# Seven products per pair of weight slabs: a new order of the products, their sums handed out one per step, and the last product in a bank of its own

## The chip, the cores and the metric

The kernel runs on one core of a Trainium2 chip. The metric is device time of one launch in microseconds (us). TensorE (PE) does the matrix products, VectorE (DVE) and ScalarE (ACT) the elementwise work, GpSimd (POOL) and SyncE (SP) issue transfers; each engine works through its own list of instructions in order.

## The reference

It is one inference step of a two-layer decoder trunk, for a prompt of 512 tokens and 8 x 8 sample tokens that share all weights (576 columns in all). Layer A is a convolution module, layer B a dilated attention. The part that matters here is the projection that feeds layer B's queries and the shared keys:

```python
h = jnp.einsum('btd,de->bte', x, w_in)        # B layer: queries, gate, memory queries, ...
q, gate, qm, gm = jnp.split(h, [MIX_WIDTH, MIX_WIDTH + B_OUT, MIX_WIDTH + B_OUT + MEM_WIDTH], axis=-1)
kv = jnp.einsum('btd,de->bte', x, w_kv_shared).reshape(b, t, 2, N_GROUPS, B_HEADS_PER_GROUP, HEAD_DIM)
```

with x of 576 x 2048 and each head a block of 128 output rows. All is float32.

## The kernel before

A product of weights by activations is done a slab at a time: 128 output rows by 2048 inputs. A slab is loaded, cast on ACT into a rounded high part `wh` (L349), and DVE takes the remainder as the low part `wl` (L360); the product is hi·hi + hi·lo + lo·hi.

Of the 24 query and key slabs of layer B, the first four are done plainly (steps `n_fill` to `n_pairs`, 16 steps of 24 matmuls), and the other 20 in ten pairs (steps `n_pairs` to `n_rest`). A pair is a 2 x 2 block product (two slabs, two halves of the 2048 inputs, two halves of 288 columns) done by Strassen's scheme in Winograd's form: seven products in place of eight, at the price of sums. The sums of the activations (tiles `comb`, made on DVE in L1173 and L1180 and on ACT in L1179) are made once, in `combine`. The sums of the weights are made for each pair: s3 = a − c (L187), s2 = d − s3 (L189), s4 = b − s2 (L193) and s1 = c + d (L197), where a and b are the two halves of the first slab and c and d those of the second; each comes in two quarters, 0 and 1, of 128 x 512.

A pair has 14 steps: 7 products, two quarters each. A step is 12 matmuls of 288 columns (L224 the eight on `wh`, L227 the four on `wl`). The results go to two PSUM tiles of two banks each: `self.x` holds the banks A and Dd, `self.y` the banks B and E. Products whose results are added stand in one bank, and what is needed before the bank goes on is copied out by `after` into the three parts s0, s1 and s2 of the tile `snap`, or is evacuated with one of them added (`ev_qk`, L1280 to L1292). `after` of a step is called at the end of the step behind it, that is behind that step's matmuls in the program.

`manual_schedule` means that each engine's instructions stand in the order in which this Python code calls them. At the end of step i, `run_steps` casts weights for the steps up to i + 3 (`issue_hi`), makes low parts up to i + 2 (`issue_split`), loads what has room (`issue_pairs`), calls `after`, and does background work from `bg` as far as the budget `state["avail"]` goes. The budget grows with the matmuls of a step and by `extra`, and is limited to `cap`. Before the pairs start, what is left of `bg` is done in one go (`while bg: one_bg()`).

The raw quarters `rawq` of a pair lie in twelve slots (eight in `qpool`, four others), loaded on SP's queue in the order of `LOADS`. Copies of caches from memory to memory (`copy_some`, L502) are also issued on SP's queue, by hooks at given steps. Behind the pairs come the value, memory and gate slabs of layer B (steps `n_rest` to `n_b`, 24 matmuls each), with sample attention beside them in a lane (`samples`), which reads cache chunks `kv` that POOL loads (L480) and whose first matmuls are in L1421.

Of the kernel before, what the change touches and what calls it, by code (L numbers as in the profile page):

```python
# [14 lines left out]
OP = mybir.AluOpType  # L15
# [66 lines left out]
def trunk(ctx, tc, xt, memt, wm, wa, wao, wb, wbo, cst, scv, kc, rest, mc, relb, oneh,  # L82
          o_y, o_yf, o_cp, o_cs, o_kv, o_kvn, o_kc, o_rest, o_mem):
    nc = tc.nc
# [56 lines left out]
    class Pair:  # L141
# [2 lines left out]


        spare = None
        LOADS = ("a0", "a1", "b0", "b1", "c0", "d0", "c1", "d1")
        PRODUCTS = (("a", "b11"), ("b", "b21"), ("s2", "t2"), ("s3", "t3"), ("s1", "t1"), ("d", "t4"), ("s4", "b22"))

        def __init__(self, slabs, move, evs, scale):  # L150
            self.slabs, self.move, self.evs, self.scale = slabs, move, evs, scale
# [22 lines left out]
        def free(self, name):  # L174
            slots[self.slot.pop(name)] += 1

        def operand(self, i):

            w, g, _ = self.sets[i]
            g = str(g)  # L180
            r = self.raw
            first = self.qi[0]
            if w == "s2" and "s3" + g not in r:
                issue_split(first + int(g) + 1)
                slots["due"] -= 1
                r["s3" + g] = n = self.take("n" + g)
                nc.vector.tensor_tensor(n, r["a" + g], r["c" + g], op=OP.subtract)  # L187
                r["s2" + g] = r.pop("a" + g)
                nc.vector.tensor_tensor(r["s2" + g], r["d" + g], n, op=OP.subtract)  # L189
            if w == "s3" and "s4" + g not in r:  # L190
                issue_split(first + 4 + int(g) + 1)
                r["s4" + g] = r.pop("b" + g)
                nc.vector.tensor_tensor(r["s4" + g], r["s4" + g], r["s2" + g], op=OP.subtract)  # L193
                self.free("a" + g)
            if w == "s1" and "s1" + g not in r:
                r["s1" + g] = r.pop("c" + g)
                nc.vector.tensor_tensor(r["s1" + g], r["s1" + g], r["d" + g], op=OP.add)  # L197
            return r[w + g]

        def done(self, i):  # L200

            w, g, _ = self.sets[i]
            slot = {"s3": "n", "s1": "c", "d": "d", "s4": "b"}.get(w)
            if slot:
                self.free(slot + str(g))

        def emit(self, i):
            if i == 0:
                self.x = new_pp()
                self.st = wpool.tile([128, 1024], F32, tag="raw", bufs=2, name=f"snap{names[0]}")  # L210
                slots["raw"] += 1
            if i == 6:
                self.y = new_pp()
            A, Dd, B, E = ((t_, c) for t_ in (self.x, getattr(self, "y", None)) for c in range(2))
            w, g, x = self.sets[i]
            t_, c = {"a": A, "b": Dd, "s2": A, "s3": B, "s1": A, "d": E, "s4": A}[w]
            hi, lo = splits[self.qi[i]]
            o = t_[:, c, 0:288]
            fresh = w in ("a", "b", "s3", "d") and g == 0
            for kk in range(4):  # L220
                if w in ("a", "b"):
                    y_ready(g * 4 + kk + (8 if w == "b" else 0), None)
                for part in range(2):
                    nc.tensor.matmul(o, hi[:, kk * 128:(kk + 1) * 128], self.move(x, g * 4 + kk, part),  # L224
                                     start=(fresh and kk == 0 and part == 0), stop=False, skip_group_check=True)
            for kk in range(4):
                nc.tensor.matmul(o, lo[:, kk * 128:(kk + 1) * 128], self.move(x, g * 4 + kk, 0), start=False,  # L227
                                 stop=(g == 1 and kk == 3), skip_group_check=True)

        def after(self, i):  # L230

            w, g, _ = self.sets[i]
            if g == 0:
                return
            sc = self.scale
            s0, s1, s2 = (self.st[:, j * 288:(j + 1) * 288] for j in range(3))
            A, Dd = (self.x[:, c, 0:288] for c in range(2))
            if w == "a":
                nc.scalar.activation(s0, A, AF.Copy, scale=sc)
            elif w == "b":  # L240
                self.evs[0](0, Dd, s0)
            elif w == "s2":
                nc.scalar.activation(s1, A, AF.Copy, scale=sc)
            elif w == "s3":
                nc.vector.scalar_tensor_tensor(s0, self.y[:, 0, 0:288], sc, s1, op0=OP.mult, op1=OP.add)
            elif w == "s1":
                nc.scalar.activation(s2, A, AF.Copy, scale=sc)
                self.evs[1](1, self.y[:, 0, 0:288], s2)
            elif w == "d":
                self.evs[1](0, self.y[:, 1, 0:288], s0)  # L250
                slots["raw"] -= 1
            else:
                self.evs[0](1, A, None)

    slots = dict(q=0, u=0, due=0, raw=0)
    steps, quarters, halves = [], [], []
# [38 lines left out]
    def issue_pairs():  # L295

        while state["dma"] < len(halves) and isinstance(halves[state["dma"]][0], Pair):
            un, name = halves[state["dma"]]
            if "q" not in scopes or slots["q"] + slots["u"] <= slots["due"] + (0 if un.raw else 2):
                return  # L300
            un.load(name)
            state["dma"] += 1
# [89 lines left out]
    def run_steps(upto=None):  # L392
        upto = len(steps) if upto is None else upto
        while state["pos"] < upto:
            i = state["pos"]
            un, q, cs, last = steps[i]
            pair = isinstance(un, Pair)
            if not pair and not hasattr(un, "ps"):
                un.ps = new_pp()
            qi = un.qi[q]  # L400
            issue_split(qi + 1)
            issue_dma(quarters[qi][2] + (6 if "s" in scopes else 4 if un.spare else 2))
            hi, lo = splits[qi]
            if pair:
                un.emit(q)
            for kk in range(0 if pair else 4):
                k = (q * 4 + kk + un.flip) % un.nk
                if un.ready:
                    for c in cs:
                        un.ready(k, c)  # L410
                w = (hi[:, kk * 128:(kk + 1) * 128], lo[:, kk * 128:(kk + 1) * 128])
                for a, (wi, xs) in enumerate(((0, un.hi), (0, un.lo), (1, un.hi))):
                    for c in cs:
                        c0, n = un.chunks[c]
                        nc.tensor.matmul(un.ps[:, c, :n], w[wi], xs[k][:, c0:c0 + n],  # L415
                                         start=(q == kk == a == 0),
                                         stop=(last and kk == 3 and a == 2 and not un.tail))
            if last and un.tail:
                un.tail(un.ps)
            state["avail"] += (288 if pair else sum(un.chunks[c][1] for c in cs)) * 12 / 2400 + state["extra"]  # L420
            for f in hooks.pop(i, []):
                f()
            top = max(v.qi[w_] for v, w_, _, _ in steps[i:i + 4]) + 1
            issue_hi(top)
            issue_split(max(v.qi[w_] for v, w_, _, _ in steps[i:i + 3]) + 1)
            if cstate["use"]:
                chunk_load()
            issue_pairs()
            if i and isinstance(steps[i - 1][0], Pair):
                steps[i - 1][0].after(steps[i - 1][1])  # L430
            elif i and steps[i - 1][3]:
                finish_evac()
            stage_lanes()
            state["avail"] = min(state["avail"], state["cap"])
            while bg and state["avail"] > 0 and (len(bg[0]) < 3 or bg[0][2]()):
                one_bg()
            state["pos"] += 1
# [1126 lines left out]
    n_rest = len(steps)  # L1564

    def samples():
        for pr in range(2):
            yield from sample_keys(pr)
            yield from sample_rest(pr)
        for pr in range(2):  # L1570
            yield from queries_mem(pr)

    first = True
# [242 lines left out]
    for i in range(16, n_out):  # L1816
        if i % 3 and not n_mk - 14 <= i < n_memkv:
            hooks.setdefault(i, []).append(copy_some)
    for i in range(n_fill + 60, n_b - 20, 5):
        hooks.setdefault(i, []).append(copy_some)  # L1820
    for j in range(8):
        hooks.setdefault(n_mk - 14 + j, []).append(lambda j=j: ld_mem(j))
# [52 lines left out]
    scopes["q"] = (ExitStack(),)  # L1875
    scopes["q"] += (scopes["q"][0].enter_context(tc.tile_pool(name="qpool", bufs=8)),)
    slots["q"] = 8
    run_steps(n_pairs)
    second_half.clear()
    while bg:  # L1880
# [1 line left out]
    state["extra"], state["cap"] = 0.0, 4.0  # L1882
    ln.clear()
    slots["u"] = 4
    run_steps(n_rest)
    assert slots["q"] == 8 and slots["u"] == 4 and not slots["due"]
    scopes.pop("q")[0].close()
    open_kv()
    cstate["limit"] = len(chunk_list)
    chunk_load()  # L1890
    lanes[1].append(samples())
    run_steps(n_b)
    drain(1)
# [131 lines left out]
```

## Time and profile before

| | us |
|---|---|
| median of 3 runs | 1827.57 (1825.32 to 1833.1) |
| the profiled execution | 1837.15 |
| its span, first to last instruction | 1835.2 |
| PE busy in the span | 1785.6 (97%) |
| DVE busy | 1125.9 (61%) |
| ACT busy | 729.4 (40%) |

The times of rows are microseconds from the span's start. A row of the timeline says start, duration, engine, line, operation, tiles (without their numbers), how many such instructions stand in a run, and in brackets how long the engine was idle before it and what ended that. Matmuls are pipelined, so that a matmul's row reaches into the next one's; the pitch from start to start counts.

### The profile page before, as it was taken

The page shows a single profiled execution, that of the slowest core. Times are in us where ns is not written, and L with a number is a line of the kernel's source. Part 1 is how long each engine was busy: PE and PEld are TensorE (multiplying, and loading weights), DVE is VectorE, ACT ScalarE, POOL GpSimd, SP SyncE. Part 2 cuts the span into 40 slices and gives each one's busy share as a digit, 9 for nine tenths or more (in the row PEclk, how much of TensorE's full clock was granted, in tenths as well). Part 3 has the DMA queues.
Part 4 walks back from the last instruction along what each step waited for, and adds up shares of the span by engine and source line. Part 5 has one row for each costly group of instructions (what it writes and reads, how often), then busy time and mean ns, then how long its engine had stood idle before and what let it go on. Part 6 is the DMA issues. An engine that isn't in the chain of part 4 may idle for free. (4 is left out here: it accounts for less than half of the span.)

```text
span 1835.2 us, 34798 instructions
## 1 busy us (share of the span) xinstructions
PE 1785.6 (97%) x14134; PEld 1700.2 (93%) x14134; DVE 1125.9 (61%) x1967; ACT 729.4 (40%) x1591; POOL 150.2 (8%) x271
## 2 busy tenths in 40 slices
PE   8999999999999999999998999999999999999998
PEld 8999999999999999999997888887888789999996
DVE  6877987478999755455877666652223322324765
ACT  5454444355455432222664443342323222334323
POOL 0222220000000000000010000011111100001000
PEclk9999999999999999999999999999999999999997
DMA  8575767565656465565751355559787786435312
GB/s 300 184 260 178 232 215 279 181 236 174 225 191 205 155 208 181 199 213 178 253 202 64 115 170 176 183 198 340 285 304 254 274 294 227 142 127 180 115 39 89
DMA packets 98751, 368.08 MB, mean 201 GB/s; under 512 B 17871, under 2 KB 27119, under 8 KB 87200
## 3 DMA queue, kind: packets, MB, share of 16 engines
q1 hardware_dynamic: 70608, 256.95, 41.6%
q0 software_dynamic: 24528, 105.76, 16.2%
q10 hardware_dynamic: 3456, 3.15, 0.5%
q8 instruction: 111, 1.82, 0.4%
q14 instruction: 48, 0.39, 0.1%
HBM read 335.02 MB, written 125.43 MB: 251 GB/s over the span
## 5 line engine op out<-in xcount | busy, mean ns | idle before, releaser
L349 ACT CAST wh<-raw 128x512 fp32r<-128x512 f32 x412 | 248.7, 617 | 371.7 <-DMA raw<-wa 129.5
L360 DVE TENSOR_TENSOR wl<-raw,wh 128x512 fp32r<-128x512 f32 x412 | 279.3, 685 | 169.5 <-ACT wh L349 85.0
L415 PE MATMUL pp<-xh,wh 128*128 128x288 f32 (+2 forms) x1408 | 307.4, 300 | 6.2 <-ACT xh L512 6.2
L415 PE MATMUL pp<-xl,wh 128*128 128x288 f32 (+2 forms) x1408 | 303.7, 298 | 0.0
L415 PE MATMUL pp<-xh,wl 128*128 128x288 f32 (+2 forms) x1408 | 303.3, 297 | 0.0
L810 DVE SCALAR_TENSOR_TENSOR conv<-ep,consts,conv 128x512 f32<-128x512 f32 x360 | 269.3, 748 | 6.9
L415 PEld LDWEIGHTS pp<-xh,wh 128*128 128x128 f32 x1408 | 234.0, 190 | 9.2 <-ACT xh L512 6.2
L415 PEld LDWEIGHTS pp<-xl,wh 128*128 128x128 f32 x1408 | 234.2, 190 | 0.3 <-DVE xl L513 0.3
L415 PEld LDWEIGHTS pp<-xh,wl 128*128 128x128 f32 x1408 | 234.3, 190 | 0.0
L415 PE MATMUL pp<-cath,wh 128*128 128x288 f32 (+2 forms) x640 | 140.5, 297 | 0.0
L415 PE MATMUL pp<-cath,wl 128*128 128x288 f32 (+2 forms) x640 | 139.7, 296 | 0.0
L415 PE MATMUL pp<-catl,wh 128*128 128x288 f32 (+2 forms) x640 | 139.5, 296 | 0.0
L415 PE MATMUL pp<-yab,wh 128*128 128x288 f32 x512 | 135.1, 306 | 0.0
L349 ACT CAST wh<-rawq 128x512 fp32r<-128x512 f32 x140 | 84.6, 619 | 122.1 <-DVE rawq L197 43.9
L224 PE MATMUL pp<-comb,wh 128*128 128x288 f32 x640 | 99.9, 298 | 15.6 <-DVE new L1292 7.8
L415 PE MATMUL pp<-yb,wh 128*128 128x288 f32 x384 | 108.0, 296 | 0.0
L224 PEld LDWEIGHTS pp<-comb,wh 128*128 128x128 f32 x640 | 89.1, 188 | 20.0 <-ACT wh L349 9.6
L415 PEld LDWEIGHTS pp<-yab,wh 128*128 128x128 f32 x512 | 91.3, 189 | 16.0 <-issue 13.0
L360 DVE TENSOR_TENSOR wl<-rawq,wh 128x512 fp32r<-128x512 f32 x140 | 95.2, 685 | 15.9 <-issue 10.2
L415 PEld LDWEIGHTS pp<-cath,wh 128*128 128x128 f32 x640 | 104.1, 189 | 0.8 <-issue 0.3
L415 PEld LDWEIGHTS pp<-cath,wl 128*128 128x128 f32 x640 | 104.0, 189 | 0.0
L415 PEld LDWEIGHTS pp<-catl,wh 128*128 128x128 f32 x640 | 104.0, 189 | 0.0
(326 smaller groups left out, 3275.9 us busy)
## 6 DMA issues: line engine op xcount, KB each, us to landing
o_kc<-kc SPq DMA_DIRECT2D x104, 512.0 KB, 5.7
kv<-kc POOLq DMA_DIRECT2D x52, 1024.0 KB, 6.9
raw<-wa SPq DMA_DIRECT2D x86, 512.0 KB, 4.3
o_rest<-rest SPq DMA_DIRECT2D x64, 512.0 KB, 6.2
raw<-wb SPq DMA_DIRECT2D x56, 512.0 KB, 5.5
rawq<-wb SPq DMA_DIRECT2D x80, 256.0 KB, 3.8
kv<-mc POOLq DMA_DIRECT2D x16, 1024.0 KB, 5.4
raw<-wao SPq DMA_DIRECT2D x32, 512.0 KB, 4.7
```

What stands on the lines that cost most here:

```text
L224: nc.tensor.matmul(o, hi[:, kk * 128:(kk + 1) * 128], self.move(x, g * 4 + kk, part), start=(fresh and kk == 0 and part == 0), stop=False, ...
L349: nc.scalar.copy(hi, r)
L360: nc.vector.tensor_tensor(lo, r, cast(hi), op=OP.subtract)
L415: nc.tensor.matmul(un.ps[:, c, :n], w[wi], xs[k][:, c0:c0 + n], start=(q == kk == a == 0), stop=(last and kk == 3 and a == 2 and not un.tail))
L810: nc.vector.scalar_tensor_tensor(cv[:, 0:TP], ep[:, k:k + TP], w, cv[:, 0:TP], op0=OP.mult, op1=OP.add)
```

## The change

In a pair the order of products becomes a, b, d, s2, s3, s1, s4: the three that need no sum stand first. The order of the loads follows. Each of the eight sums now has a step at whose end it is issued (table `SUMS`; -1 is the step before the pair), where before the sums of a product were made by the call that cast its first weights. The last product s4 goes to the bank Dd, which b's evacuation has left, and what s1 left in A is copied out to s2 and added when s4 is evacuated; before it went on in A. The second tile is taken at step 4 instead of 6.

Around this, the background work gets `extra` 1.2 and `cap` 4.0 in the last ten of the plain steps; the cache copies are hooked to each fourth step from the first pair on, where they were hooked to each fifth from some way into the pairs to near the end of the stage behind; the first cache chunks' loads stand one step earlier, and the lane of sample attention starts two steps later.

```diff
-        LOADS = ("a0", "a1", "b0", "b1", "c0", "d0", "c1", "d1")
-        PRODUCTS = (("a", "b11"), ("b", "b21"), ("s2", "t2"), ("s3", "t3"), ("s1", "t1"), ("d", "t4"), ("s4", "b22"))
+        LOADS = ("a0", "c0", "a1", "b0", "d0", "b1", "c1", "d1")
+        PRODUCTS = (("a", "b11"), ("b", "b21"), ("d", "t4"), ("s2", "t2"), ("s3", "t3"), ("s1", "t1"), ("s4", "b22"))
+        SUMS = {-1: "s30", 1: "s20", 2: "s31", 3: "s21", 5: "s10", 6: "s11", 7: "s40", 8: "s41"}
...
+        def sum(self, name):
+            w, g = name[:2], name[2]
+            r = self.raw
+            if w == "s3":
+                slots["due"] -= 1
+                r[name] = self.take("n" + g)
+                nc.vector.tensor_tensor(r[name], r["a" + g], r["c" + g], op=OP.subtract)
+            elif w == "s2":
+                issue_split(self.qi[0] + int(g) + 1)
+                r[name] = r.pop("a" + g)
+                nc.vector.tensor_tensor(r[name], r["d" + g], r["s3" + g], op=OP.subtract)
...
         def emit(self, i):
-            if i == 6:
+            if i == 4:
                 self.y = new_pp()
-            A, Dd, B, E = ((t_, c) for t_ in (self.x, getattr(self, "y", None)) for c in range(2))
+            A, Dd, E, B = ((t_, c) for t_ in (self.x, getattr(self, "y", None)) for c in range(2))
             w, g, x = self.sets[i]
-            t_, c = {"a": A, "b": Dd, "s2": A, "s3": B, "s1": A, "d": E, "s4": A}[w]
+            t_, c = {"a": A, "b": Dd, "s2": A, "s3": B, "s1": A, "d": E, "s4": Dd}[w]
...
             elif w == "s3":
-                nc.vector.scalar_tensor_tensor(s0, self.y[:, 0, 0:288], sc, s1, op0=OP.mult, op1=OP.add)
+                nc.vector.scalar_tensor_tensor(s1, self.y[:, 1, 0:288], sc, s1, op0=OP.mult, op1=OP.add)
+                self.evs[1](0, self.y[:, 0, 0:288], s1)
             elif w == "s1":
                 nc.scalar.activation(s2, A, AF.Copy, scale=sc)
-                self.evs[1](1, self.y[:, 0, 0:288], s2)
-            elif w == "d":
-                self.evs[1](0, self.y[:, 1, 0:288], s0)
+                self.evs[1](1, self.y[:, 1, 0:288], s2)
+            elif w == "s4":
+                self.evs[0](1, Dd, s2)
                 slots["raw"] -= 1
-            else:
-                self.evs[0](1, A, None)
...
+            if pair:
+                un.sums(q)
+            if i + 1 < len(steps) and isinstance(steps[i + 1][0], Pair) and steps[i + 1][1] == 0:
+                steps[i + 1][0].sums(-1)
...
     def samples():
+        for _ in range(2):
+            yield 0.0
...
-    for i in range(n_fill + 60, n_b - 20, 5):
+    for i in range(n_pairs, n_rest - 8, 4):
         hooks.setdefault(i, []).append(copy_some)
...
+    run_steps(n_fill + 6)
+    state["extra"], state["cap"] = 1.2, 4.0
     run_steps(n_pairs)
...
-    run_steps(n_rest)
+    run_steps(n_rest - 1)
     assert slots["q"] == 8 and slots["u"] == 4 and not slots["due"]
     scopes.pop("q")[0].close()
     open_kv()
     cstate["limit"] = len(chunk_list)
     chunk_load()
+    run_steps(n_rest)
```

On DVE, between the first products of one pair, the order was, before (`rawq` on the left is the sum made, `wl` a low part, `qk` b's evacuation):

```order
L187 TENSOR_TENSOR rawq650_11667<-rawq638_11444,rawq645_11524 128x512
L189 TENSOR_TENSOR rawq638_11444<-rawq646_11543,rawq650_11667 128x512
L360 TENSOR_TENSOR wl338_11672<-rawq637_11425,wh338_11651 128x512
L193 TENSOR_TENSOR rawq639_11446<-rawq639_11446,rawq637_11425 128x512
L360 TENSOR_TENSOR wl339_11690<-rawq638_11444,wh339_11670 128x512
L193 TENSOR_TENSOR rawq641_11467<-rawq641_11467,rawq638_11444 128x512
L360 TENSOR_TENSOR wl340_11709<-rawq649_11648,wh340_11688 128x512
L1282 SCALAR_TENSOR_TENSOR qk654_11715<-pp648_11615,snap648_11616 128x72x4
```

and is now, at the same place (L186 is s3, L190 s2, L194 s1):

```order
L190 TENSOR_TENSOR rawq653_11732<-rawq657_11791,rawq663_11890 128x512
L369 TENSOR_TENSOR wl352_11945<-rawq657_11791,wh352_11926 128x512
L186 TENSOR_TENSOR rawq665_11947<-rawq655_11770,rawq659_11813 128x512
L369 TENSOR_TENSOR wl353_11964<-rawq660_11815,wh353_11943 128x512
L190 TENSOR_TENSOR rawq655_11770<-rawq660_11815,rawq665_11947 128x512
L369 TENSOR_TENSOR wl354_11983<-rawq653_11732,wh354_11962 128x512
L1295 SCALAR_TENSOR_TENSOR qk667_11985<-pp664_11892,snap664_11893 128x72x4
L369 TENSOR_TENSOR wl355_12001<-rawq655_11770,wh355_11981 128x512
L194 TENSOR_TENSOR rawq654_11751<-rawq654_11751,rawq657_11791 128x512
L369 TENSOR_TENSOR wl356_12020<-rawq663_11890,wh356_11999 128x512
```

A low part now stands between any two sums.

On PE, the rows of a pair at which a step's first matmul waits for another engine were, before, from the second product on (`yh` is the product b and s4, `comb` the others; pp648 is the tile x, pp656 the tile y):

```order
L224 MATMUL pp648_11615<-yh552_10672,wh336_11611 128x288 [waits Activation_49]
...
L224 MATMUL pp648_11615<-yh563_10829,wh337_11629 128x288 [waits Activation_49]
...
L224 MATMUL pp648_11615<-comb609_11292,wh339_11670 128x288 [waits DVE_49]
...
L224 MATMUL pp656_11736<-comb579_11022,wh344_11769 128x288 [waits DVE_49,Activation_49]
...
L224 MATMUL pp656_11736<-comb611_11296,wh345_11787 128x288 [waits DVE_49,Activation_49]
```

These are the steps b0, b1, the second step of s2, and the two steps of d. Now the steps b0, b1, the first of s2, and the two of s4 read (pp692 is x):

```order
L234 MATMUL pp692_12433<-yh552_10672,wh378_12427 128x288 [waits Activation_49]
...
L234 MATMUL pp692_12433<-yh563_10829,wh379_12448 128x288 [waits Activation_49]
...
L234 MATMUL pp692_12433<-comb575_10984,wh382_12503 128x288 [waits DVE_49,Activation_49]
...
L234 MATMUL pp692_12433<-yh552_10672,wh388_12622 128x288 [waits Activation_49]
...
L234 MATMUL pp692_12433<-yh563_10829,wh389_12642 128x288 [waits Activation_49]
```

The products a and b still follow each other in x, and s1 and s4 now do; b and s2, which did, are two steps apart, and so are the two products in y.

On DVE at the head of the stage the order was, before, from the low part of the pair's second step on (`comb` is background work of which 14 more rows like these stand here):

```order
L360 TENSOR_TENSOR wl_11287<-rawq_11133,wh_11250 128x512
L1173 TENSOR_TENSOR comb_11289<-r_9556,r_8510 128x288
L1173 TENSOR_TENSOR comb_11289<-r_9556,comb_11258 128x288
L1180 TENSOR_TENSOR comb_11293<-comb_11258,comb_11292 128x576
...
L1180 TENSOR_TENSOR comb_11339<-comb_11331,comb_11338 128x576
L360 TENSOR_TENSOR wl_11362<-rawq_11135,wh_11285 128x512
```

and is now:

```order
L369 TENSOR_TENSOR wl_11308<-rawq_11162,wh_11264 128x512
L1193 TENSOR_TENSOR comb_11311<-comb_11275,comb_11310 128x576
L369 TENSOR_TENSOR wl_11340<-rawq_11166,wh_11306 128x512
L186 TENSOR_TENSOR rawq_11342<-rawq_11162,rawq_11164 128x512
L369 TENSOR_TENSOR wl_11365<-rawq_11168,wh_11338 128x512
```

The first row of each fence but the last is that of the second step; in the last fence it is that of the pair's first step, and only one `comb` row stands behind it.

## Rows read from the trace of the kernel before

**Rows 1.** Who waited for whom on PE: total us, times, longest us.
```profile
PE pp L224 <- ACT snap L239: 8.3, 10, 3.8
PE pp L224 <- DVE new L1292: 7.8, 9, 1.1
PE pp L224 <- DVE qk L1282: 7.0, 10, 0.7
PE pp L227 <- DVE wl L360: 3.3, 1, 3.3
```
**Rows 2.** Busy us by stretch: length, PE, PEld, DVE, ACT, POOL, clock, DMA share, GB/s.
```profile
970.00:992.00 22.00, 14.14 (x90) 13.45 (x89) 18.38 (x35) 8.72 (x15) 0.54 (x1) 0.84 0.19 61
992.00:1232.00 240.00, 220.60 (x1614) 214.42 (x1613) 153.65 (x269) 93.92 (x175) 17.02 (x32) 1.00 0.48 158
...
1240.00:1244.00 4.00, 3.48 (x17) 2.29 (x18) 0.00 (x0) 0.00 (x0) 0.55 (x1) 0.63 1.01 419
```
**Rows 3.** Timeline of a pair of the middle, step by step.
```profile
1023.71 1.23 PE L224 MATMUL pp<-comb,wh 128*128 128x288 f32 x8
1023.90 0.41 ACT L247 ACTIVATE snap<-pp 128x288 f32<-128x288 f32 x1 [1.49 <-PE pp L227]
...
1026.31 1.30 PE L224 MATMUL pp<-comb,wh 128*128 128x288 f32 x8 [0.85 <-DVE new L1292]
...
1031.19 1.22 PE L224 MATMUL pp<-yab,wh 128*128 128x288 f32 x8
...
1034.37 0.29 PE L224 MATMUL pp<-yh,wh 128*128 128x288 f32 x1
...
1035.42 0.69 PE L227 MATMUL pp<-yh,wl 128*128 128x288 f32 x4
...
1036.14 0.41 ACT L239 ACTIVATE snap<-pp 128x288 f32<-128x288 f32 x1
...
1036.61 0.40 PE L224 MATMUL pp<-yh,wh 128*128 128x288 f32 x1 [0.50 <-ACT snap L239]
...
1038.30 1.23 PE L224 MATMUL pp<-comb,wh 128*128 128x288 f32 x8
...
1039.36 0.69 PE L227 MATMUL pp<-comb,wl 128*128 128x288 f32 x4
1040.09 0.65 DVE L1282 SCALAR_TENSOR_TENSOR qk<-pp,snap 128x288 f32<-128x288 f32 x1 [1.61 <-PE pp L227]
...
1040.79 1.33 PE L224 MATMUL pp<-comb,wh 128*128 128x288 f32 x8 [0.74 <-DVE qk L1282]
```
**Rows 4.** Timeline of PE: start of the first pair, the second pair, the stage behind.
```profile
972.43 1.23 PE L224 MATMUL pp<-yab,wh 128*128 128x288 f32 x8
...
1006.07 1.22 PE L224 MATMUL pp<-yab,wh 128*128 128x288 f32 x8
...
1231.77 0.42 PE L415 MATMUL pp<-yh,wh 128*128 128x288 f32 x2
...
1240.52 1.45 PE L1421 MATMUL at<-kv,qe 128*32 128x512 f32 x8 [2.19 <-issue]
```
**Rows 5.** Timeline of DVE at the head of the stage.
```profile
943.60 0.45 DVE L1173 TENSOR_TENSOR comb<-r 128x288 f32<-128x288 f32 x1
...
970.02 0.45 DVE L1173 TENSOR_TENSOR comb<-r 128x288 f32<-128x288 f32 x1
...
973.13 0.45 DVE L1173 TENSOR_TENSOR comb<-r 128x288 f32<-128x288 f32 x1
...
979.38 0.69 DVE L360 TENSOR_TENSOR wl<-rawq,wh 128x512 fp32r<-128x512 f32 x1
```
**Rows 6.** Timeline of POOL: the first cache chunks.
```profile
1231.08 1.09 POOL L480 DMA_DIRECT2D kv<-kc  x2 [0.25 <-issue]
```
**Rows 7.** DMA issues on SP: how many, KB each, median us to landing.
```profile
o_kc<-kc SPq DMA_DIRECT2D x104, 512.0 KB, 5.7
rawq<-wb SPq DMA_DIRECT2D x80, 256.0 KB, 3.8
```

More of the change, by code (lines that the diff above doesn't have):

```diff
@@ L175, in free @@
             slots[self.slot.pop(name)] += 1
+        def sum(self, name):
[9 more added lines that the diff above has]
+                nc.vector.tensor_tensor(r[name], r["d" + g], r["s3" + g], op=OP.subtract)
+            elif w == "s1":
+                issue_split(self.qi[4] + int(g) + 1)
+                r[name] = r.pop("c" + g)
+                nc.vector.tensor_tensor(r[name], r[name], r["d" + g], op=OP.add)
+                self.free("d" + g)
+            else:
+                issue_split(self.qi[6] + int(g) + 1)
+                r[name] = r.pop("b" + g)
+                nc.vector.tensor_tensor(r[name], r[name], r["s2" + g], op=OP.subtract)
+                self.free("a" + g)
@@ L177, in operand, with sums @@
+        def sums(self, i):
+            if i in self.SUMS:
+                self.sum(self.SUMS[i])
         def operand(self, i):
             w, g, _ = self.sets[i]
[L180 to L198, printed above, removed]
+            return self.raw[w + str(g)]
@@ L200, in done @@
         def done(self, i):
             w, g, _ = self.sets[i]
-            slot = {"s3": "n", "s1": "c", "d": "d", "s4": "b"}.get(w)
+            slot = {"s3": "n", "s1": "c", "s4": "b"}.get(w)
             if slot:
@@ L211, in emit @@
                 slots["raw"] += 1
-            if i == 6:
+            if i == 4:
                 self.y = new_pp()
-            A, Dd, B, E = ((t_, c) for t_ in (self.x, getattr(self, "y", None)) for c in range(2))
+            A, Dd, E, B = ((t_, c) for t_ in (self.x, getattr(self, "y", None)) for c in range(2))
             w, g, x = self.sets[i]
-            t_, c = {"a": A, "b": Dd, "s2": A, "s3": B, "s1": A, "d": E, "s4": A}[w]
+            t_, c = {"a": A, "b": Dd, "s2": A, "s3": B, "s1": A, "d": E, "s4": Dd}[w]
             hi, lo = splits[self.qi[i]]
             o = t_[:, c, 0:288]
-            fresh = w in ("a", "b", "s3", "d") and g == 0
+            fresh = w in ("a", "b", "s3", "d", "s4") and g == 0
             for kk in range(4):
```

## The prediction

> **What bounds the kernel now.** PE is busy 97% of the span, so only its idle time and the time that it spends at the lower clock can be won. I read first who waited for whom on PE [rows 1]: the four largest waits inside the pairs are three kinds of evacuation, ten, nine and ten times, and one low part at their start; together 26.4 us. The busy time by stretch [rows 2] puts this in place: from 992 to 1232, in the pairs, PE is busy 220.6 of 240 us at full clock, with DVE busy 154 us and the DMA engines half busy; from 970 to 992, at the head of the stage, it is busy 14.1 of 22 us, at a granted clock of 0.84. Last I read the timeline of one pair and of the head [rows 3 to 5].
>
> How long a step is without a wait: the two steps of product a run from 1031.19 to 1034.37 [rows 3], 1.59 us each; fourteen are 22.3 us. The first pair starts at 972.43, the second at 1006.07, the stage behind at 1231.77 [rows 4]. So the first pair takes 33.6 us, 11.4 more than its steps, and the other nine (1231.77 − 1006.07) / 9 = 25.1 us each, 2.8 more.
>
> Where the 2.8 us stand is seen in the starts of steps [rows 3]. From the first to the second step of b it is 1036.61 − 1034.37 = 2.24 us, of s2 1040.79 − 1038.30 = 2.49, of d 1026.31 − 1023.71 = 2.60; less 1.59 these are 0.65, 0.90 and 1.01, together 2.56, and the step behind each is about 0.1 late as well (1036.61 to 1038.30 is 1.69). All three have one cause, and the rest turns on it. DVE sits idle 1.61 us and starts b's evacuation at 1040.09, although b was complete before 1038.30: the matmuls that end at 1039.36 + 0.69 = 1040.05 are the first step of s2, which writes the *other bank of the same tile*. Then the second step of s2 waits for that evacuation. The same at a and b: the snapshot of a starts at 1036.14, when b's first step ends (1035.42 + 0.69), and b's second step starts at 1036.61, when the snapshot is over. But the snapshot of s1 starts at 1023.90, 0.2 us into the first step of d, which writes the other tile. So a read of a tile waits for the matmuls that stand ahead of it in the program in either bank of that tile, and later ones wait for the read. The evacuation of a product is issued behind the first step of the next one. It costs PE a stop wherever two neighbours of the order stand in one tile: a and b (x, x), b and s2 (x, x), s1's evacuation and d (y, y). Three per pair.
>
> **The change, part by part.** *Order and banks.* The new order is a, b (x), d (y), s2 (x), s3 (y), s1 (x), s4 (x), then the next pair's a in the tile that y has left. Neighbours in one tile: a and b as before, and now s1 and s4. b's evacuation, 0.65 us on DVE, now runs beside the steps of d and is awaited two steps later, by s2; d needs no evacuation of its own any more until s3 is done, and that runs beside s1. So two of three stops go (s2's and d's: 0.90 + 1.01 and their 0.1 each, 2.1 us) and one comes: the snapshot of s1 is issued behind the first step of s4 in x, waits for its end, and the second step waits for the snapshot. That wait is the same as the one at a and b: an ACT copy of 0.41 us [rows 3], so 0.65 + 0.1 = 0.75 us. Two such stops are left, 1.5 us, and a pair takes 23.8 us. Bounds of the new stop: none, if a bank's read does not wait for the other bank; 1.1 us, what the dearest stop of before costs. I take the middle one since it is the same instruction in the same position. Nine pairs: 9 x (2.8 − 1.5) = **11.7 us**.
>
> Behind the new snapshot stand, on ACT, the casts for the next pair's b, wanted three steps later, and on DVE the evacuation of y (0.54 and 0.20 us), for which the next pair's a waits, as it takes y's place. It ends about 1.3 us after s4's first step, while s4's second starts 0.5 us after it and takes 1.6: hidden, with 0.8 us to spare. s4 is evacuated by DVE with an addition in place of ACT: ten times 0.74 us more on DVE, less 0.2, with the stretch's DVE at 64% [rows 2].
>
> *Sums.* Eight per pair as before, each now one step or more before its cast. At 0.69 us a sum and 0.69 a low part no step holds more than one of each plus an evacuation of 0.65, 2.0 us in one step of 1.59, with lighter ones on both sides; low parts are made two steps ahead. I cost this at nothing; if that cover were gone, a late low part would cost what it is late, once a pair.
>
> *Head of the stage.* Before, DVE gets the background's last rounds in one go: a round is 973.13 − 970.02 = 3.11 us, and the low part of b's first step comes at 979.38 [rows 5], for which PE stands 3.3 us, and then 3.8 for a's snapshot, which queues behind the casts that wait for sums [rows 1]; the stops bring the clock down [rows 2]. Now eight rounds go beside the last ten plain steps, from 943.60 on. They are 8 x 3.11 = 24.9 us, ten low parts about 6, evacuations 0.7: 31.6 us, to about 975, less the last 0.7 us of it, which stands behind a's low part. PE wants that at 972.43 + 1.06. I take 1 us of waiting (0 to 4: none, or what is left of today's first stop and some queue on ACT). With its two stops the first pair is 1.5 + 1 = 2.5 us over its steps in place of 11.4: **8.9 us**.
>
> *Behind the pairs.* The first cache chunk is issued at 1231.08 [rows 6] and its first use starts at 1240.52 after 2.19 us of idle [rows 4]; then the clock is at 0.63 for 4 us, in which PE is busy 3.5 [rows 2]: (1 − 0.63) x 3.5 = 1.3 us more. With the lane two steps (6 us) later and the load within about 1 us of where it was, this wait is over: **3.5 us** (0, if the waits only move to the next chunk; 5, if later waits shrink too).
>
> *Copies.* 21 copies either way; they now start with the first pair, 3.5 of 512 KB in a pair in place of 2.8, on SP's queue among the loads. A load of 256 KB lands in 3.8 us, a copy in 5.7 (median) [rows 7], and the loads are issued seven steps or so (11 us) ahead of their sums. Nothing.
>
> Sum: 11.7 + 8.9 + 3.5 = 24.1 us. Against the profiled execution's own 1837.15 (1.95 of it outside the span) that is 1813.1. The median of the runs is 9.6 us below that execution; taken off the median, 1827.57 − 24.1 = **1803.5**.
>
> **The rivals.** *Both snapshots are free.* If reads wait bank by bank, all stops go: 9 x 2.8 + (11.4 − 1) + 3.5 = 39.1 us, 1788.5. For it: different banks are written and read. Against it: the two starts at 1040.09 and 1036.14 above. The Trainium skill (PSUM — Partial Sum Buffer, Summary: rules for kernel authors) says to guard PSUM reads by bank, and to read another bank than the one that matmuls fill; by that rule this rival's time would come out. The trace does not agree: these waits are by tile.
>
> *Only the pairs gain.* If DVE is still behind at the head (its work there fills the ten steps to the brim) and the cache's wait only moves on, 11.7 us are left, less up to 2: about 1816 to 1818.
>
> *No change.* The sums don't come in time after all, and a low part stands late in each pair by about the 1.3 us that the banks give: within 9 us of before, about 1822. For it: DVE, in order, stands at each evacuation until a product ends. Against it: 64% busy, two steps of lead.
>
> *Slower.* Loads late behind copies. Place: the sum s3 of the next pair, which DVE meets in the last step of a pair, needs a quarter that SP issues behind up to three copies; if it hasn't landed, DVE stands, and with it the low parts queued behind. It decides from a landing later than about 11 us; to end 9 us above before it must cost 33 us, 3.3 in each of ten pairs: 1837. Against it: 3.8 us to land, DMA half busy [rows 2, 7]. The skill (Trainium Kernel Development and Optimization, Key Constraints) says that transfers of all queues run on the same 16 DMA engines and interleave, which speaks for this rival; the trace shows those engines with half their time free in this stretch.
>
> **How the numbers follow.** Forecast 0.66; both free 0.07; only the pairs 0.14; no change 0.08; slower 0.05. A measurement of this kernel tells about 0.5% (9.1 us) from no change: below 1818.4 is faster. The forecast, the first rival and two thirds of the second are faster, 0.82; the rest of the second and the third are the same, 0.13; slower 0.05. The forecast's own range is 1796 to 1812 (the new stop 0 to 1.1 us a pair, the head 0 to 4, the stage behind 0 to 5). The range that leaves out no more than two in ten runs from 1790, nearly the first rival, to 1817, most of the second.
>
> **What would show it.** Right: pairs 23.6 to 24.0 us from a to a; in each just two stops of PE, both for an ACT snapshot, before b's and s4's second steps, and none for DVE; the 3.3 and 3.8 us at the head gone, with a wait of 0 to 4 us for a low part near it, and the granted clock near 1 there; no stop at the first cache chunk. Wrong: a pair of 22.3 us (no stop at s4: waits by bank), a low part's wait that comes back in each pair (sums too late), DVE's idle before a sum ended by a transfer (loads late), or a new stop at the start of a (y's evacuation late).

## The result and the profile after

The changed kernel takes 1806.77 us (median of 4 runs, 1805.46 to 1814.14), where the kernel before beside it takes 1827.76: a ratio of 0.989, 95% interval 0.9855 to 0.9924. The forecast was 1803.5. The profiled execution of after takes 1805.46 us, with a span of 1803.6.

The starts of the same matmuls in the two profiled executions, counted from the program's first, tell where the time went (us; each stage holds the same matmuls in both kernels, and only their order inside a pair and behind the pairs differs):

```
                                            before    after   after - before
up to the first pair                        972.43   968.35    -4.08
the first pair                               33.64    23.80    -9.84
nine pairs                                  225.70   214.19   -11.51
stage behind, to the 12,501st matmul        365.14   367.17    +2.03
  of it the first 72 matmuls                 13.51    16.44
to the 14,001st                             200.81   200.81     0.00
to the last, the 14,134th                    32.34    24.01    -8.33
```

The row of the first 72 matmuls has no difference, since it counts the same number and not the same work: in the kernel before, eight of them are sample attention's, which now come later.

Two rows are not the change's. Of the 4.08 us, 3.6 stand ahead of the ten plain steps in which the two programs first differ, and the other 0.5 is less than the 1.0 us by which these ten steps differ between the executions of before and of e10 (below), which are the same program there. And at the end the same instructions run at the lower of the clock's two levels in the execution of before (0.50 of full is 1.2 GHz), at the full one in that of after. The busy times by stretch show the end (length, PE, PEld, DVE, ACT, POOL, clock, DMA share, GB/s); before first, then after:

```profile
1811.00:1831.00 20.00, 19.47 (x45) 10.65 (x44) 7.97 (x23) 7.72 (x16) 0.00 (x0) 0.50 0.34 125
```
```profile
1788.00:1799.00 11.00, 10.61 (x43) 5.88 (x41) 7.33 (x22) 7.70 (x15) 0.00 (x0) 1.00 0.59 215
```

The runs of one kernel spread in the same way (of the four of after, three take 1805 to 1807 us at a mean granted clock of 0.995 to 0.997, and one 1814 at 0.990), so that such an end is the likely reason why medians of one kernel differ by several us between groups of runs, though only the profiled executions show where the clock was low. So terms are compared below by the starts of matmuls, stage by stage. The change's own part is 9.84 + 11.51 − 2.03 = 19.3 us.

Who waited for whom on PE, after (total us, times, longest). It answers to [rows 1]: the two DVE waits and the low part's wait inside the pairs are gone, two ACT waits of 0.50 us a pair are left, and two lines for the stage behind (L358, L369) are new.

```profile
PE pp L234 <- ACT snap L249: 5.0, 10, 0.5
PE pp L234 <- ACT snap L258: 5.0, 10, 0.5
PE pp L424 <- ACT wh L358: 3.3, 1, 3.3
PE at L1434 <- DMA kv<-kc: 3.0, 3, 2.3
PE pp L424 <- DVE wl L369: 2.4, 3, 1.2
```

Busy times by stretch of after: the first pair, the nine others, the first 72 matmuls behind them. They answer to [rows 2]: the head now runs at full clock, the stage behind starts at 0.79.

```profile
968.35:992.15 23.80, 22.80 (x170) 22.33 (x169) 18.19 (x33) 11.54 (x23) 1.08 (x2) 1.00 0.46 167
992.15:1206.34 214.19, 205.15 (x1514) 200.97 (x1513) 147.80 (x264) 84.46 (x155) 15.35 (x29) 1.00 0.47 161
1206.34:1222.78 16.44, 11.90 (x74) 11.32 (x73) 4.21 (x10) 2.47 (x6) 2.40 (x5) 0.79 0.69 223
```

The timeline of after around the end of one pair and the start of the next, to be read against [rows 3]: at 1013.77 the snapshot of s1 starts, when s4's first step in the same tile has ended (1013.04 + 0.69), and s4's second step stands 0.50 us for it; at 1020.91 and 1021.37 the same at a and b. At 1023.25 DVE evacuates b while d runs in the other tile, and nobody waits.

```profile
1013.04 0.69 PE L237 MATMUL pp<-yh,wl 128*128 128x288 f32 x4
1013.77 0.41 ACT L258 ACTIVATE snap<-pp 128x288 f32<-128x288 f32 x1 [3.04 <-PE pp L237]
...
1014.23 0.41 PE L234 MATMUL pp<-yh,wh 128*128 128x288 f32 x1 [0.50 <-ACT snap L258]
...
1020.91 0.41 ACT L249 ACTIVATE snap<-pp 128x288 f32<-128x288 f32 x1 [3.08 <-PE pp L237]
...
1021.37 0.40 PE L234 MATMUL pp<-yh,wh 128*128 128x288 f32 x1 [0.50 <-ACT snap L249]
...
1023.25 0.68 DVE L1295 SCALAR_TENSOR_TENSOR qk<-pp,snap 128x288 f32<-128x288 f32 x1 [0.70 <-PE pp L237]
```

The new stop behind the pairs: PE's timeline, then DVE's, SP's and ACT's, all of after.

```profile
1206.34 0.42 PE L424 MATMUL pp<-yh,wh 128*128 128x288 f32 x2
...
1216.23 0.61 PE L424 MATMUL pp<-yab,wh 128*128 128x288 f32 x1 [3.33 <-ACT wh L358]
...
1218.77 0.61 PE L424 MATMUL pp<-yab,wl 128*128 128x288 f32 x1 [1.21 <-DVE wl L369]
```
```profile
1206.60 0.69 DVE L369 TENSOR_TENSOR wl<-raw,wh 128x512 fp32r<-128x512 f32 x1
...
1218.63 0.55 DVE L1295 SCALAR_TENSOR_TENSOR qk<-pp,snap 128x224 f32<-128x224 f32 x1
```
```profile
1207.35 12.28 SPq L338 DMA_DIRECT2D raw<-wb  x2
```
```profile
1215.57 0.62 ACT L358 CAST wh<-raw 128x512 fp32r<-128x512 f32 x1 [9.67 <-DMA raw<-wb]
```

The load at 1207.35 is the second half of the first slab behind the pairs, and PE wants it about 6.4 us (two steps) after that stage's start. The load goes out 1.01 us after the start, and ACT, which casts it for PE, stands idle until it has landed. In the kernel before the same load went out 2.24 us ahead of the start (1231.77 in [rows 4]), as DVE's evacuation at 1228.77 ended:

```profile
1229.53 0.33 SPq L329 DMA_DIRECT2D raw<-wb  x1
```
```profile
1228.77 0.69 DVE L1282 SCALAR_TENSOR_TENSOR qk<-pp,snap 128x288 f32<-128x288 f32 x1 [0.84 <-PE pp L227]
```

The load also takes longer to land: 8.1 us, where it took 5.2 before and takes 3.7 in experiment 4. The rows show that load alone, of after, before and e4 (KB, us from issue to landing):

```profile
raw<-wb SPq DMA_DIRECT2D x1, 512.0 KB, 8.1
raw<-wb SPq DMA_DIRECT2D x1, 512.0 KB, 5.2
raw<-wb SPq DMA_DIRECT2D x1, 512.0 KB, 3.7
```

In after it is on its way beside the first cache chunks, with the DMA engines 0.79 to 0.98 busy from 1206.3 to 1215. Had it landed in 5.2 us, about 3.33 − (8.1 − 5.2) = 0.4 us of the first wait would be left. So by this estimate most of that wait needs the longer landing as well as the late start; that the chunks make the landing longer is likely, but was not tested.

The snapshot tile `snap` of a pair and the half slabs `raw` share two places (tag `raw`, `bufs=2`). Before, the last pair's snapshot was given up with d's evacuation, and the load went into its place. Now s4's evacuation reads the snapshot too and gives it up one product later (`slots["raw"] -= 1` moved; the evacuation is the row at 1218.63); so the load takes the place of the slab's first half, which is free when its second low part is made (1206.60 + 0.69). That the place held longer, and not the later lane or the copies, makes the stop is what experiments 2 and 4 test.

### The profile page after: what moved, and what is told of

Read it like the earlier page. It is cut to its first block, busy times and chain, and to the rows that moved or that the text cites. A ratio compares the mean times of both kernels' runs of the same rounds, so it can differ in the third digit from the quotient of the medians.

```text
span 1803.6 us, 34789 instructions
## 1 busy us (share of the span) xinstructions
PE 1771.4 (98%) x14134; PEld 1691.3 (94%) x14134; DVE 1127.7 (63%) x1977; ACT 724.6 (40%) x1581; POOL 150.3 (8%) x271
## 4 chain that ended last, share of the span: by engine, by line
PE 92%; DMA 4%; DVE 1%; ACT 1%; issue 1%; ACTq 0%; POOL 0%; SPq 0%; DVEq 0%; POOLq 0%
PE pp L424 69%; PE pp L234 8%; PE pp L237 4%; DMA kv<-kc 2%; PE at L1489 1%; DMA raw<-wb 1%; PE at L1434 1%; PE at L619 1%; PE at L597 1%; DMA raw<-wa 1%; PE at L1371 1%; PE at L1369 1%; PE at L664 0%; PE at L644 0%; PE at L612 0%
## 5 line engine op out<-in xcount | busy, mean ns | idle before, releaser
L358 ACT CAST wh<-raw 128x512 fp32r<-128x512 f32 x412 | 248.5, 617 | 366.4 <-DMA raw<-wa 149.8
L369 DVE TENSOR_TENSOR wl<-raw,wh 128x512 fp32r<-128x512 f32 x412 | 279.4, 685 | 153.1 <-ACT wh L358 76.7
L369 DVE TENSOR_TENSOR wl<-rawq,wh 128x512 fp32r<-128x512 f32 x140 | 95.8, 687 | 28.3 <-PE pp L237 17.2
L358 ACT CAST wh<-rawq 128x512 fp32r<-128x512 f32 x140 | 84.6, 620 | 65.0 <-PE pp L234 61.4
L796 ACT ACTIVATE prod<-es,consts 128x64 f32<-128x64 f32 x360 | 102.9, 343 | 1.2 <-ACT mkv L564 1.2
L424 PE MATMUL pp<-yh,wh 128*128 128x288 f32 x448 | 100.0, 305 | 0.0
```

What stands on the lines that cost most here:

```text
L358: nc.scalar.copy(hi, r)
L369: nc.vector.tensor_tensor(lo, r, cast(hi), op=OP.subtract)
L796: nc.scalar.activation(dst, es[:, :, k:k + 8], AF.Copy, scale=w)
```

## The experiments

Each ratio is to the kernel before on the same chip, whose median was 1833.76 us beside e1 to e4, 1826.81 beside e5 to e8 and 1826.27 beside e9 and e10; so ratios are to be compared, not medians. The stages come from the profiled executions. Pairs, the stage behind them (to the 12,501st matmul) and its first 72 matmuls in us (in e8 and e10, as in the kernel before, eight of the 72 are sample attention's, so this column does not compare those two with the others):

```
                          median   ratio to before [95%]      1st pair  9 pairs   stage  72 mm
after                     1806.77  0.989  [0.9855, 0.9924]     23.80    214.19   367.17  16.44
e5 after again            1813.8   0.9916 [0.9884, 0.9948]     23.79    214.18   365.89  16.50
e1 one-bank tiles         1791.15  0.9787 [0.9755, 0.982]      22.26    200.41   365.89  15.87
e2 old pair               1814.9   0.991  [0.9881, 0.994]      27.94    226.03   358.95   9.57
e3 no extra, cap          1814.24  0.9904 [0.9876, 0.9933]     30.08    214.19   368.51  15.45
e4 snapshot given up      1802.18  0.9833 [0.9805, 0.9861]     23.79    214.19   359.23   9.57
e6 e1 and e4              1787.17  0.9776 [0.9744, 0.9808]     22.26    200.40   358.65   9.58
e7 e2 and one-bank tiles  1783.81  0.977  [0.9737, 0.9802]     22.75    199.97   358.30   9.41
e8 e6, lane as before     1793.33  0.9812 [0.9777, 0.9846]     22.26    200.40   362.91  14.07
e9 e6, copies as before   1785.66  0.9764 [0.9729, 0.9799]     22.26    200.40   360.31   9.58
e10 before, e1's tiles    1803.34  0.9845 [0.9797, 0.9893]     28.97    199.98   365.54  10.58
```

**1. Are the stops the chip's or the program's?** Edit (y likewise):

```diff
-                self.x = new_pp()
+                self.x = [at(), at()]
...
-            o = t_[:, c, 0:288]
+            o = t_[c][:, 0:288]
...
```

> The changed kernel with the pair's four banks as four one-bank tiles in place of two two-bank tiles; nothing else differs. Theory (the two ACT stops a pair are waits for the other bank of the same tile, which the program makes, not the chip): both stops of 0.50 us go, a pair takes 22.3 to 22.6 us in place of 23.80, ten pairs gain 12 to 15 us, the time is 1792 to 1795 against 1806.8. Rival (the stops are of the chip: a bank cannot be read while PE fills its neighbour): the pair stays at 23.8 and the time within 3 us of 1806.8. Second rival (another wait takes their place, DVE's evacuations or low parts): a pair of 23 us with stops of another name, 1799.

Measured: both stops are gone, and in nine pairs PE has no idle time at all. First the busy times of the nine pairs, then a piece of the timeline of the same kernel:

```profile
991.42:1191.83 200.41, 200.41 (x1515) 200.41 (x1514) 149.66 (x263) 86.23 (x155) 15.92 (x30) 1.00 0.50 172
```
```profile
1038.62 0.69 PE L237 MATMUL at<-yab,wl 128*128 128x288 f32 x4
1039.15 0.29 PE L234 MATMUL at<-yh,wh 128*128 128x288 f32 x1
1039.28 0.29 PE L234 MATMUL at<-yl,wh 128*128 128x288 f32 x1
1039.34 0.41 ACT L249 ACTIVATE snap<-at 128x288 f32<-128x288 f32 x1 [1.50 <-PE at L237]
```

The snapshot of a now starts when a ends (1038.62 + 0.69), beside the matmuls of b in the next bank, and neither waits. So the chip does not need these stops. The program asked for them, since its waits are set by tile and a tile was two banks. The Trainium skill (PSUM — Partial Sum Buffer, Summary: rules for kernel authors) says to guard reads by bank and to read another bank than the one being filled; with one bank to a tile the trace agrees: 0 us of waiting in 200.41.

**2. The old pair in the changed surroundings.** Edit: `LOADS`, `PRODUCTS`, the sums, the banks and `after` as before; `extra` and `cap`, copies, lane and cache loads stay changed.

> The changed kernel with the pair as it was before (order of products, sums, banks); the head's extra and cap, the copies and the later lane stay changed. Prediction's first term: a steady pair is 25.1 us again with three stops of two DVE kinds and one ACT kind, so 11.5 us come back in nine pairs and about 1 to 2 in the first. If the stop behind the pairs comes from the snapshot tile being given up one product later, it is gone here and gives back 2 to 6 us: 1814 to 1819 in all. Rival (that stop is from the later lane or the earlier cache load): it stays, 1819 to 1821. Rival (the pair's gain needs the spread of sums and more is lost): above 1822.

Measured: steady pairs of 25.1 us, 2.8 us over that in the first pair, and no stop behind the pairs: the load goes out 2.24 us ahead of the stage's start at 1220.51.

```profile
1218.27 2.32 SPq L329 DMA_DIRECT2D raw<-wb  x2
```

The stage takes 358.95 us in place of 367.17. So the new stop comes with the pair's change, and without it the rest of the change gains 365.14 − 358.95 = 6.2 us in this stage.

**3. The head.** Edit:

```diff
-    run_steps(n_fill + 6)
-    state["extra"], state["cap"] = 1.2, 4.0
```

> The changed kernel without extra 1.2 and cap 4.0 in the last ten plain steps. Prediction's second term (these settings won the head): DVE gets the last rounds of the background in one go again, the first pair's low parts come late, and the 8.9 us of the head come back, 1814 to 1817; the first pair takes 31 to 35 us. Rival (the new order won it, since its first three products want no sums): only a low part is late, 3 to 5 us with the slower clock behind it, 1810 to 1812, first pair 27 to 29 us. Second rival (the rounds in one go cost nothing now): 1806.8.

Measured: between the first expectation and its rival. The first pair takes 6.3 us more than in after. The low part's wait of the kernel before [rows 1] is back; the one for the snapshot is no longer than anywhere. PE's timeline and the clock there (last row: stretch):

```profile
977.97 1.33 PE L237 MATMUL pp<-yh,wl 128*128 128x288 f32 x4 [3.89 <-DVE wl L369]
979.80 0.61 PE L234 MATMUL pp<-yh,wh 128*128 128x288 f32 x1 [0.50 <-ACT snap L249]
```
```profile
970.00:985.00 15.00, 10.61 (x62) 10.03 (x62) 14.03 (x27) 8.06 (x15) 0.54 (x1) 0.77 0.34 107
```

With e2 this splits the head. Over a steady pair of its own kernel the first one takes 8.6 us more in the kernel before, 2.8 with the settings alone (e2), 6.3 with the order alone (e3), 0 with both (after).

**4. The snapshot given up early**, in the last pair. Edit:

```diff
+            if i == 10 and self.last:
+                self.st2 = u([128, 288], name="snap")
...
+            if self.last:
+                s2 = self.st2
...
                 self.evs[1](0, self.y[:, 0, 0:288], s1)
+                slots["raw"] -= 1 if self.last else 0
...
                 self.evs[0](1, Dd, s2)
-                slots["raw"] -= 1
+                slots["raw"] -= 0 if self.last else 1
...
+    steps[-1][0].last = True
```

> The changed kernel; in the last pair alone the third part of the snapshot lies in a tile of its own, so that the tile of the other two is given up when s3 is evacuated, and the second half of the first slab behind the pairs is loaded into its place, about 6 us earlier. Theory (that load, issued 1.0 us behind the stage's start where before it was 2.2 us ahead, makes the new stop): the waits of 3.33 us for the high part and 1.2 for the low part go and the half clock behind them, 72 matmuls from the stage's start take 9.6 to 11 us in place of 15.7, and the time falls by 4 to 6 us to 1801 to 1803. Rival (the stage is bound by its cache chunks, DMA engines 0.9 to 1.0 busy there): the stop goes, but waits for cache chunks grow by as much, 1805 to 1807.

Measured: as the theory says. SP's load goes out at 1201.12, 5.7 us ahead of the stage's start (1206.81), behind the evacuation that now frees the place; PE does not stop in the first 72 matmuls, and the stage takes 359.23 us, 6.7 to 7.9 less than in the two executions of after.

```profile
1200.38 0.68 DVE L1300 SCALAR_TENSOR_TENSOR qk<-pp,snap 128x288 f32<-128x288 f32 x1
```
```profile
1201.12 7.04 SPq L343 DMA_DIRECT2D raw<-wb  x2
```
```profile
1206.81:1216.38 9.57, 9.57 (x74) 9.57 (x73) 5.05 (x14) 3.08 (x8) 2.40 (x5) 1.00 0.94 313
```

**5 and 6. The changed kernel again, and the edits of 1 and 4 together.**

> The changed kernel itself once more, beside the three others on the same chip, so that they have it as their base: pairs of 23.79 us, 15 to 16.5 us for the first 72 matmuls of the stage behind the pairs, 1804 to 1810.

Its pairs are there again within 0.02 us and its stop within 0.1, and the stage behind differs by 1.3. Its median is above the 1804 to 1810 expected and 7 us above the first group's. Three of its six runs have a mean granted clock of 0.988 to 0.990, as one of the first group's four has, but no trace shows where in them the clock was low: its profiled execution, at 1804.07 us, is not one of them.

> The changed kernel with both mends: four one-bank tiles per pair and the last pair's snapshot tile given up early. If the two costs are apart from each other they add up: pairs of 22.27 us, 72 matmuls behind them in 9.6 us, the stage behind about 8 us shorter than in the changed kernel; 22 to 23 us under the changed kernel, 1784 to 1786 if that is at 1807. Rival (without the stops the pairs come up against the next limit, loads or low parts, or the stage behind meets its cache chunks earlier and waits for them): 15 to 19 us under it.

The two costs add up: from the first pair's start to the 12,501st matmul 581.3 us, against 605.2 and 603.9 in the two executions of after, 22.5 to 23.8 less. All ten pairs run without a gap:

```profile
970.44:1193.11 222.67, 222.67 (x1683) 222.67 (x1681) 168.25 (x296) 99.00 (x180) 17.00 (x32) 1.00 0.51 176
```

**7. Is the new order needed?** Edits of 1 and 2 together.

> The changed kernel with the pair as it was before (old order, old sums), but four one-bank tiles per pair; head, copies and lane stay changed. Theory (the order was worth time only since neighbours shared a tile): a steady pair takes 22.3 to 22.6 us in the old order too, only the first pair is about 2.8 us over its steps, no stop behind the pairs; 1 to 4 us above the kernel with both mends, about 1787. Rival (with no stops to hide in, the old sums, made by the call that casts, bring low parts late): pairs of 23 to 24 us, 8 to 17 us above it.

```profile
994.51:1194.48 199.97, 199.97 (x1514) 199.97 (x1513) 146.36 (x255) 87.56 (x164) 16.23 (x31) 1.00 0.52 173
```

Measured: no. In the old order, with the sums made by the casting call, the pairs run without a gap too, 22.22 us each, and the first is 0.5 over, where 2.8 were expected. The kernels e6 and e7 are not told apart (0.9776 and 0.977, intervals overlapping; 581.3 and 581.0 us from the first pair to the 12,501st matmul): the new order with its sums, which were only changed together, was worth time only as long as a tile was two banks.

**8 and 9. What the stage behind gained.** Edits, each on e6: the two yields at the start of `samples` taken out; the hooks of the copies as before.

> The kernel with both mends, but the lane of sample attention starts two steps earlier, where it stood before. The third term of the prediction (the later lane takes the wait at the first cache chunk away): a wait of 2 to 3 us for a chunk near the stage's start comes back, with slow clock behind it up to 4 us in all, 2 to 4 us above the kernel with both mends. Rival (the earlier load or the copies did it; or later chunks give the time back since the stage moves at the pace of its chunks): within 1 us of it.

> The kernel with both mends, but the cache copies hooked where they stood before (each fifth step from some way into the pairs to near the end of the stage behind). The prediction costs the move of the copies at nothing: pairs of 22.27 us and within 1 us in the stage behind. Rival (the stage behind, whose DMA engines are 0.9 to 1.0 busy, gains by having none): the stage behind takes 1 to 4 us more, by waits for cache chunks.

Without the later lane the stop at the first cache chunk of [rows 4] is back (waits on PE in this stage of e8):

```profile
PE at L1439 <- issue: 2.7, 1, 2.7
```

and the stage takes 4.3 us more than in e6. With the old copies the pairs stay at 22.27 us, as forecast; the stage takes 1.7 us more, which is the rival's range and not the 1 us forecast, and the waits for cache chunks grow from 2.7 us (e6) to 4.4 (e9; second fence):

```profile
PE at L1439 <- DMA kv<-kc: 2.7, 3, 1.8
```
```profile
PE at L1439 <- DMA kv<-kc: 4.4, 5, 2.6
```

1.7 us is little more than the 1.3 by which the stage differs between the two executions of after, and the medians do not show it (ratio 0.9764 against 0.9776 for e6), so this size is rough.

**10. The kernel before with one-bank tiles alone.**

> The kernel before with four one-bank tiles per pair and nothing else. If the stops were all that the old order cost, its steady pairs take 22.2 us; the head keeps what late sums and low parts cost there (first pair 28 to 31 us), and the stage behind keeps its wait for the first cache chunk: 25.1 - 22.2 = 2.9 us in nine pairs, 26 us, and 2 to 5 at the head, 1797 to 1800 against 1827.6, so the changed kernel's whole gain is surpassed by the banks alone.

The stages came as expected, 22.22 and 28.97 us; its profiled execution ended at the lower clock (31.96 us from the 14,001st matmul to the last, where after takes 24.01), and its median of 1803.34 is above the range of 1797 to 1800. By stages it is 594.5 us from the first pair to the 12,501st matmul, 9 to 11 less than after.

## Why the prediction came out nearly right

**Pairs: right, in size and mechanism.** Forecast 23.8 us a pair with two ACT stops and no DVE stop, measured 23.79 and the two stops; 11.5 us in nine pairs where 11.7 were forecast. The reading that a read waits for what stands ahead of it in either bank of its tile, and that s1's snapshot would meet s4's first step in this way, is shown by 1013.77 and 1014.23 above and by e1. What the prediction did not say is that the cause can be lifted without any new order: it held the rival of reads that wait bank by bank against the trace and let the trace decide. As a forecast of this change that was right; as a statement on the chip it would have been wrong.

**Sums at no cost: right.** No sum or low part is late in a steady pair; with PE never idle (e1) DVE is busy 149.66 of 200.41 us, 75%, and still in time. But handing the sums out one per step is not what keeps them in time: with the old sums no gap stands in a steady pair either (e7, e10).

**Head: size right (9.8 us against 8.9), reason half right.** The last 1 us did not come: the first pair takes no more than any other. But the prediction gave the whole to `extra` and `cap`. They alone win 5.7 (e2); without them 6.3 come back (e3); the rest needs products without sums at the front, or, by e7, tiles of one bank.

**Behind the pairs: wrong, and outside the term's own bounds of 0 to 5.** Forecast 3.5 us gained, measured 2.0 lost (0.8 by the second execution, e5): without the new stop the stage gains 6.2 (e2), and the stop costs more than that. The step that failed is not the one on the lane, which took the wait for the first chunk away and is worth 4.3 us (e8). It is the step on order and banks, which costed s4's evacuation with an addition as DVE time only. That addition reads the snapshot, so the snapshot's tile is held one product longer; its place was the one that the next stage's second half slab had been loaded into. The load went out 3.25 us later against the stage's start and took 2.9 longer to land, PE waited 3.33 and 1.21 us, and its granted clock fell to the lower level (0.50 from 1215 to 1220): 6.7 to 7.9 us (e4). A place held longer costs nothing in the pairs, where none but the snapshots wants it, and shows at the first load behind them.

**Copies: right in the pairs**, where they cost nothing, and rough in the stage behind, where their absence is worth some 1.7 us (e9).

**Rivals.** That both snapshots are free did not come, since the program still waits by tile; e1 is what the pairs would then have been like: by stages it gains 11.4 us in the first pair and 25.3 in the nine others, near the 10.4 and 25.2 worked out for this rival. Late loads did not come: the quarters land later than in [rows 7] (the page of after: KB, median us to landing), but the longest takes 7.9 us, short of the 11 from which that rival decides, and no sum stood for one. Nor are the copies most of it: the median is 3.9 us with the old pair beside the moved copies (e2), and 4.8 against 5.1 with the new pair and the copies as before (e9, e6).

```profile
rawq<-wb SPq DMA_DIRECT2D x80, 256.0 KB, 5.2
```

The sum was 24.1 us and the change's own part is 19.3. Of the 4.8 us between them, the stage behind is 5.5 too high, the head 0.9 too low and the pairs 0.2 too high. The forecast is 3.3 us below the measured median, and that it is no further off is luck in part: medians of few runs differ by some us in code that did not change, and that of the same kernel in e5, 1813.8, lies outside the forecast's own range of 1796 to 1812, though inside that of 1790 to 1817.

## What to carry to other kernels

When PE stops for an evacuation of a product that has long been done, look at which tile the matmuls in between write: if it is another bank of the same tile, give each bank a tile of its own before reordering any work (here 15 us in one edit, and the old order was then as good as the new). When a change makes a late instruction read an old buffer, follow that buffer's place past the end of the loop: ask who is loaded into it next, and when that load is wanted. Then look at what else is being transferred when it goes out: here a load 3.25 us later also took 2.9 longer. Compare two profiled executions by the starts of the same matmuls, so that stages without a change drop out, and see first that a stretch holds the same ones in both.

## What the runs showed of the hardware

ACT and DVE read one bank of PSUM while PE fills another without any time lost on PE (200.41 of 200.41 us busy in e1). And the last 44 matmuls, the same instructions with PE busy 19.47 of 20 us in the execution of before and 10.61 of 11 in that of after, ran at a granted clock of 0.50 in the one and 1.00 in the other, 8.3 us apart, though PE had been busy 16.00 of 16.00 us at 1.00 just ahead in both; what decides between the two was not tested.
